# An encoder layer in one kernel: one weight unit of the merges split in front of the first long chunk's fifth job instead of its first

## The chip, the core and the metric

The kernel runs on one core of a Trainium2 chip. The core has a matrix engine (TensorE, PE in the profile; its weight loads are PEld), a vector engine (VectorE, DVE), a scalar engine (ScalarE, ACT), a general engine (GpSimd, POOL) and a queue engine (SyncE, SP) that here does nothing but issue transfers between the chip's memory and the on-chip buffers. Sixteen DMA engines carry the transfers. Each engine takes its instructions strictly in a written order and waits at an instruction until its inputs, and the buffer it writes, are ready.

The metric is the device time of one execution in microseconds, lower is better.

## The reference

One layer of a hybrid encoder over two sequences, a prompt of 1024 tokens and a sample of 2048, each with 16 learned tokens in front, 1024 channels wide, all in float32:

```python
xn = _rmsnorm(h, g_pre)
proj = xn @ w_in + b_in
na_q, na_k, na_v, na_z, ml_qk, ml_v, ml_z, ml_o, ml_g, mg = jnp.split(proj, SPLIT_IDX, axis=-1)
ya = _neighbourhood_attention(na_q, na_k, na_v, na_rpb)
ya = (ya * jax.nn.silu(na_z)) @ w_a
yb = (_mlstm_branch(ml_qk, ml_v, ml_g, ml_o, ml_conv_w, ml_head_g) * jax.nn.silu(ml_z)) @ w_b
ga, gb = jnp.split(jax.nn.sigmoid(mg), 2, axis=-1)
y = (ga * ya + gb * yb) @ w_out
return h + _rmsnorm(y, g_post)
```

So there is one wide input projection; from its columns come a neighbourhood attention on a grid of 64 columns (8 heads of 64) and a bidirectional mLSTM in chunks of 64 tokens (4 heads of 128, with a short convolution in front of its q and k); the two results are gated, projected, mixed and sent through `w_out`.

## The kernel before

**Products.** A float32 matrix is carried as two parts, a high part (`xh`, or the first half of `whl`) and a low part (`xl`, or the second half), and a product is three matmuls: high by high, high by low, low by high. For features on the partitions these are lines 218 to 220, for tokens on the partitions lines 787 to 789.

**Weight units.** The weights come in units of up to 128 x 1056 numbers. On its first use a unit is split: the raw unit is loaded (line 289, `wraw<-wu`, 0.5 MB, two buffers), ACT copies its high part (line 317), DVE subtracts to get the low part (line 318), both into one buffer `whl` of four that go round (`NBW` is 4), and the pair is stored to memory (line 341, `w_...<-whl`, 1 MB). On a later use the stored pair is loaded (line 310, `whl<-w_...`, 1 MB). The number after `w_` only names the stored pair. The core of the split, and the branch for a unit that is split ahead of its use:

```python
both = wp.tile([P, 2, 4 * WU], F32R, name="whl", bufs=NBW)
...
nc.sync.dma_start(both[:, :, :n].bitcast(F32), self.wkept[key])
...
nc.scalar.activation(hi[:, c], raw[:, c], AF.Copy)
nc.vector.tensor_tensor(lo[:, c], raw[:, c], hi[:, c].bitcast(F32), op=ALU.subtract)
...
if key in self.ahead:
    self.wrdy.append(None)
```

A unit that is split ahead is not used by the job that follows: it takes a buffer, is stored, and the buffer is free for the next unit once the store has read it. Such units are the weights of the last stages, here called the merges: the list `MERGE[:-5]`, eleven of them.

**Stages and jobs.** `PLAN` has thirteen dense stages. The first two work on the prompt, the third and fourth on the two halves of the sample ("long chunks" of 1024 tokens; `j` is 2 and 3), then follow the rest of the projections and six merges. A long chunk has nine jobs, `layout("mv")`: two with features on the partitions (four units each: mLSTM q, then mLSTM z), six with tokens on the partitions (two units each: twice 264 columns wide, four times 256), and the mLSTM k's again with four units. `requests` writes the list of units in the order in which they are fetched; in front of some jobs it puts in one unit of the merges.

**Tokens on the partitions.** `tm_unit` takes both units of its job at once and runs tile after tile: 12 matmuls with the first unit (4 blocks of 128 channels by three), then 12 with the second, then DVE adds the bias row `bb` (lines 803 and 805).

**Order.** The dense work above is interleaved with the mLSTM and the attention of the stages already projected. TensorE's order is written out. The orders of DVE, ACT, POOL and SP are set at build time by a scheduler from a model of times; so a changed list of units can also reorder other rows of these engines. Other names used below: `xr<-x_sample` (line 408) loads the sample for its norm, `xsq<-xr` (line 365) sums its squares; `kth` and `ktl` (lines 1577 and 1578) are the two parts of an mLSTM key; `raw<-mk`, `um<-ud`, `gg<-stT`, `to<-stT` and `va<-mv` are loads and stores of the mLSTM and its inputs, `xh<-xh` and `xl<-xl` loads or stores of the two parts of a normed chunk.

Of the kernel before, what the change touches and what calls it, by code (L numbers as in the profile page):

```python
# [57 lines left out]
def _weight_units():  # L58

    return ([("i", x, P) for x in FM_COLS] + [("t", *c, a) for c in TM_COLS for a in range(2)]  # L60
            + [("m", f, P) for f in range(KT)] + [("o", c, a) for c in range(4) for a in range(2)])


def _sw_order(pairs):

    seq = [(pairs[0], "11")]
    for i, p in enumerate(pairs):
        mid = ("22", "s1") if i == 0 else ("s1", "22")
        seq += [(p, o) for o in ("12", "s2", "s3") + mid]
        if i + 1 < len(pairs):  # L70
            seq.append((pairs[i + 1], "11"))
        seq.append((p, "s4"))
    return seq
# [65 lines left out]
class K:  # L139
# [725 lines left out]
    def requests(self):  # L865

        unit = {k: j for j, k in enumerate(_weight_units())}
        ahead = deque(MERGE[:-5])
        self.ahead, first = set(ahead), True
        for j, (s, t0, cols) in enumerate(PLAN):  # L870
            if s == "f":
                assert not ahead
                keys = MERGE[:-5] + [None] * first + MERGE[-5:]
                first = False
            else:
                keys = []
                if "g" not in cols:
                    for n, (kind, c) in enumerate(self.layout(cols)):
                        if ahead and (j == 2 and n < 4 or j == 3 and n):
                            keys.append(ahead.popleft())  # L880
                        keys += [("i", x, P) for x in c] if kind == "fm" else [("t", *c, a) for a in range(2)]
                else:
                    assert not ahead
                    pairs = [p for p in range(14) if "ng"[p > 5] in cols]
                    lead = pairs if (s, t0) not in SW else self.lead(j)
                    keys = [("q", (p, f + "1"), (p, f + "2")) for p in lead for f in "12"]
                    pairs = [p for p in pairs if p not in lead]
                    if pairs:
                        seq = _sw_order(pairs)
                        keys += [("q", *seq[x:x + 2]) for x in range(0, len(seq), 2)]  # L890
            for k in keys:
                if k is None:
                    self.wreq.append(None)
                    continue
                if k[0] == "q":
                    self.wreq.append((k, None, KT, P))
                    continue
                nk, w = (KT, P) if k[0] in "im" else (4, k[2] if k[0] == "t" else 256)
                self.wreq.append((k, self.i["wu"][unit[k], :, :nk * w], nk, w))
# [1307 lines left out]
```

## Time and profile before

| quantity | value |
|---|---|
| median of 3 runs | 2666.21 us (2662.89 to 2666.56) |
| profiled execution | 2665.67 us, span 2663.9 us |
| mean granted TensorE clock | 0.997 |
| PE busy | 2635.1 us, 99% of the span |
| DVE, ACT, POOL busy | 1915.0, 1423.7, 196.3 us |
| memory traffic | 800.47 MB, mean 300 GB/s |

The span runs from the first to the last instruction of the profiled execution. Busy time is counted per engine; an idle engine is of no interest by itself. In the rows of the trace a bracket gives how long the engine was idle before an instruction and what it then waited for. The granted clock is the share of full speed at which TensorE was let run; a value of 0.5 in a short window means that matmuls there took twice as long.

### The profile page before, as it was taken

The page shows a single profiled execution, that of the slowest core. Times are in us where ns is not written, and L with a number is a line of the kernel's source. Part 1 is how long each engine was busy: PE and PEld are TensorE (multiplying, and loading weights), DVE is VectorE, ACT ScalarE, POOL GpSimd, SP SyncE. Part 2 cuts the span into 40 slices and gives each one's busy share as a digit, 9 for nine tenths or more (in the row PEclk, how much of TensorE's full clock was granted, in tenths as well). Part 3 has the DMA queues.
Part 4 walks back from the last instruction along what each step waited for, and adds up shares of the span by engine and source line. Part 5 has one row for each costly group of instructions (what it writes and reads, how often), then busy time and mean ns, then how long its engine had stood idle before and what let it go on. Part 6 is the DMA issues. An engine that isn't in the chain of part 4 may idle for free.

```text
span 2663.9 us, 46683 instructions
## 1 busy us (share of the span) xinstructions
PE 2635.1 (99%) x15928; PEld 2328.5 (87%) x15928; DVE 1915.0 (72%) x5070; ACT 1423.7 (53%) x3292; POOL 196.3 (7%) x418
## 2 busy tenths in 40 slices
PE   9999999999999999999999999999999999999998
PEld 7898897899988999878888888878889898989888
DVE  5655678788776877546676776857478889797854
ACT  5423555555445554546665676656366655656521
POOL 0111131011301124000000000000000000000000
PEclk9999999999999999999999999999999999999999
DMA  9899988799866999978889998899899899898965
GB/s 371 328 332 337 332 302 303 279 339 344 313 218 242 352 324 309 317 230 268 261 269 342 370 295 260 282 348 324 275 323 321 283 306 286 284 306 266 326 244 206
DMA packets 393517, 800.47 MB, mean 300 GB/s; under 512 B 50528, under 2 KB 173360, under 8 KB 389440
## 3 DMA queue, kind: packets, MB, share of 16 engines
q1 hardware_dynamic: 361728, 697.24, 77.9%
q0 software_dynamic: 31552, 100.25, 10.2%
q8 instruction: 126, 2.06, 0.3%
q14 instruction: 111, 0.91, 0.1%
HBM read 543.72 MB, written 253.60 MB: 299 GB/s over the span
## 4 chain that ended last, share of the span: by engine, by line
PE 91%; DMA 4%; DVE 3%; ACT 1%; issue 1%; SPq 0%; DVEq 0%; ACTq 0%
PE pj L218 10%; PE pj L220 10%; PE pj L219 10%; PE pj L988 8%; PE pj L990 8%; PE pj L989 8%; PE pj L787 5%; PE pj L789 5%; PE pj L788 5%; PE pj L1954 3%; PE pj L1953 3%; PE pj L1955 3%; PE sm L1288 3%; PE tr L1273 2%; PE sm L220 1%; PE sm L219 1%
## 5 line engine op out<-in xcount | busy, mean ns | idle before, releaser
L218 PE MATMUL pj<-xh,whl 128*128 128x512 f32 (+1 forms) x960 | 369.7, 385 | 3.1 <-ACT xh L445 2.5
L220 PE MATMUL pj<-xh,whl 128*128 128x512 f32 (+1 forms) x960 | 361.0, 376 | 0.0
L219 PE MATMUL pj<-xl,whl 128*128 128x512 f32 (+1 forms) x960 | 360.3, 375 | 0.2 <-DVE xl L446 0.2
L787 PE MATMUL pj<-whl,xh 128*128 128x256 f32 (+1 forms) x1152 | 329.0, 286 | 0.0
L789 PE MATMUL pj<-whl,xl 128*128 128x256 f32 (+1 forms) x1152 | 325.3, 282 | 0.0
L788 PE MATMUL pj<-whl,xh 128*128 128x256 f32 (+1 forms) x1152 | 324.9, 282 | 0.0
L1953 PE MATMUL pj<-whl,mh 128*128 128x256 f32 x768 | 218.3, 284 | 1.1 <-DMA whl<-w 1.1
L787 PEld LDWEIGHTS pj<-whl,xh 128*128 128x128 f32 x1152 | 217.1, 188 | 0.4
L788 PEld LDWEIGHTS pj<-whl,xh 128*128 128x128 f32 x1152 | 217.0, 188 | 0.2
L789 PEld LDWEIGHTS pj<-whl,xl 128*128 128x128 f32 x1152 | 217.0, 188 | 0.0
L1954 PE MATMUL pj<-whl,mh 128*128 128x256 f32 x768 | 216.3, 282 | 0.0
L1955 PE MATMUL pj<-whl,mlo 128*128 128x256 f32 x768 | 215.5, 281 | 0.0
L218 PEld LDWEIGHTS pj<-xh,whl 128*128 128x128 f32 x960 | 181.2, 189 | 35.3 <-ACT xh L445 3.4
L220 PEld LDWEIGHTS pj<-xh,whl 128*128 128x128 f32 x960 | 181.2, 189 | 35.0
L219 PEld LDWEIGHTS pj<-xl,whl 128*128 128x128 f32 x960 | 181.8, 189 | 30.4 <-issue 1.0
L988 PE MATMUL pj<-xh,whl 128*128 128x512 f32 x512 | 206.7, 404 | 1.3 <-ACT pj L1005 1.1
L990 PE MATMUL pj<-xh,whl 128*128 128x512 f32 x512 | 202.0, 395 | 0.0
L989 PE MATMUL pj<-xl,whl 128*128 128x512 f32 x512 | 201.1, 393 | 0.0
L1280 DVE TENSOR_TENSOR pts<-tr,pts 96x384 fp32r<-96x384 f32 (+2 forms) x192 | 118.6, 618 | 63.8 <-ACT pts L1275 62.4
L1275 ACT ACTIVATE pts<-tr 96x384 fp32r<-96x384 f32 (+2 forms) x192 | 103.5, 539 | 101.7 <-PE tr L1273 101.1
L218 PE MATMUL pj<-yh,whl 128*128 128x512 f32 x384 | 154.1, 401 | 0.0
L219 PE MATMUL pj<-yl,whl 128*128 128x512 f32 x384 | 151.5, 395 | 0.7 <-DVE yl L1855 0.7
(380 smaller groups left out, 6824.9 us busy)
## 6 DMA issues: line engine op xcount, KB each, us to landing
whl<-w SPq DMA_DIRECT2D x131, 1024.0 KB
whl<-q SPq DMA_DIRECT2D x112, 512.0 KB
w<-whl SPq DMA_DIRECT2D x36, 1024.0 KB
wraw<-wu SPq DMA_DIRECT2D x48, 512.0 KB
gt<-st SPq DMA_DIRECT2D x96, 256.0 KB
tg<-gt SPq DMA_DIRECT2D x96, 256.0 KB
q<-po POOLq DMA_DIRECT2D x26, 512.0 KB, 7.3
xt<-xt SPq DMA_DIRECT2D x24, 512.0 KB
```

The lines of the kernel that those rows point to most:

```text
L218: mm(out, ah, bh, start=start, stop=False)
L219: mm(out, ah, bl, start=False, stop=False)
L220: mm(out, al, bh, start=False, stop=stop)
L787: nc.tensor.matmul(o, xh, wh, start=k == 0, stop=False)
L788: nc.tensor.matmul(o, xh, wl, start=False, stop=False)
L789: nc.tensor.matmul(o, xl, wh, start=False, stop=k == KT - 1)
L988: mm(bank, w[:, 0, k], xh[:, k], start=fresh and k == 0, stop=False, skip_group_check=True)
L989: mm(bank, w[:, 0, k], xl[:, k], start=False, stop=False, skip_group_check=True)
L990: mm(bank, w[:, 1, k], xh[:, k], start=False, stop=k == 3, skip_group_check=True)
L1953: nc.tensor.matmul(o, mh[:, k, xs], wh, start=clear > 0 and k == 0, stop=False)
L1954: nc.tensor.matmul(o, mh[:, k, xs], wl, start=False, stop=False)
L1955: nc.tensor.matmul(o, ml[:, k, xs], wh, start=False, stop=clear < 2 and k == KT - 1)
```

## The change

Of the nine jobs of the first long chunk (`j == 2`), four have a merge unit split in front of them. Before, these were the first four jobs; after, they are the second to the fifth. The second long chunk (`j == 3`) keeps its seven. The list of merge units, what is computed from them and the order of TensorE's matmuls stay as they are; the four units are each split one job later.

```diff
@@ -876,7 +876,7 @@
                 keys = []
                 if "g" not in cols:
                     for n, (kind, c) in enumerate(self.layout(cols)):
-                        if ahead and (j == 2 and n < 4 or j == 3 and n):
+                        if ahead and (j == 2 and 0 < n < 5 or j == 3 and n):
                             keys.append(ahead.popleft())
                         keys += [("i", x, P) for x in c] if kind == "fm" else [("t", *c, a) for a in range(2)]
                 else:
```

Two stretches of SP's queue differ by it. The first is the boundary in front of the first long chunk, where a split is taken out; `w_305` is the first unit of that chunk's first job. The piece of the difference:

```order
 L1507 DMA va_2774<-mv_246 128x2x128
-L408 DMA xr<-x_sample 128x1024 x4
+L408 DMA xr<-x_sample 128x1024
+L310 DMA whl<-w_305 128x2x1024
+L408 DMA xr<-x_sample 128x1024 x3
 L415 DMA xt<-xt 128x1024
 L723 DMA nz_151<-st 128x512
-L415 DMA xt<-xt 128x1024
+L1507 DMA va_2774<-mv_246 128x2x128
 L1620 DMA kf<-kf_189 128x256
-L341 DMA w_5198<-whl 256x1x1024
-L289 DMA wraw<-wu 128x1024
```

The store of the split and the raw load of the unit after it are gone from here, and the load of `w_305`, which stood further down, is now the second row behind `va`, among the loads of the sample.

The second stretch is SP's queue around the end of the first long chunk's third job. `w_1411` and `w_1434` are the two units of its fifth job (256 columns). Before:

```order
L310 DMA whl<-w_1411 128x2x1024
L310 DMA whl<-w_1434 128x2x1024
L766 DMA bb<-b_in 128x256
L830 DMA to_257<-stT 128x2x264
L562 DMA xh_512_5658<-xh 128x512
L1437 DMA raw<-mk_207 128x257
L827 DMA gg_259<-stT 128x2x16
L830 DMA to_257<-stT 128x2x248
L562 DMA xh_512_5658<-xh 128x512
L1626 DMA um<-ud_265 128x2x128
L1626 DMA um<-ud_266 128x2x128
L827 DMA gg_259<-stT 128x2x16
```

After, the same stretch begins with these rows:

```order
L310 DMA whl<-w_1411 128x2x1024
L341 DMA w_6986<-whl 256x1x1024
L289 DMA wraw<-wu 128x1024
L766 DMA bb<-b_in 128x256
L830 DMA to_257<-stT 128x2x264
L562 DMA xh_512_5651<-xh 128x512
L827 DMA gg_259<-stT 128x2x16
L830 DMA to_257<-stT 128x2x248
L562 DMA xh_512_5651<-xh 128x512
L1437 DMA raw<-mk_207 128x257
```

and goes on with these, the last rows of the stretch that matter:

```order
L1626 DMA um<-ud_265 128x2x128
L1626 DMA um<-ud_266 128x2x128
L827 DMA gg_259<-stT 128x2x16
L562 DMA xh_512_5651<-xh 128x512
L562 DMA xl_512_5652<-xl 128x512
L830 DMA to_257<-stT 128x2x248
L1507 DMA va_2774<-mv_246 128x2x128
L310 DMA whl<-w_1434 128x2x1024
```

Where the load of `w_1434` stood there are now the store of a split (`w_6986`) and the raw load of the next unit, and the load of `w_1434` stands sixteen rows behind the store, with `raw<-mk_207` halfway. On DVE the split itself comes in at the same place:

```order
-L641 TENSOR_TENSOR xr<-xh,xl 128x1024
-L1657 TENSOR_TENSOR q_6999<-cv,q_6999 128x2x128
-L641 TENSOR_TENSOR xr<-xh,xl 128x1024
+L641 TENSOR_TENSOR xr<-xh,xl 128x1024 x2
+L318 TENSOR_TENSOR whl<-wraw,whl 128x1024
 L805 TENSOR_TENSOR stT<-pj,bb 128x264
 L1673 TENSOR_TENSOR um<-um,trim 128x256
```

The subtraction of line 318 now stands behind both `xr` pieces and ahead of the bias addition, and `q` has moved behind it.

## The prediction

> **What bounds the kernel now.** I read the page's totals first, then TensorE's waits, then the chain of work, and last the rows of the two places where the order differs. Columns of the timeline rows: start in us, duration in us, engine, line, operation, out<-in, shapes; in brackets the idle time before it and its releaser.
>
> ```profile
> span 2663.9 us, 46683 instructions
> PE 2635.1 (99%) x15928; PEld 2328.5 (87%) x15928; DVE 1915.0 (72%) x5070; ACT 1423.7 (53%) x3292; POOL 196.3 (7%) x418
> ```
>
> TensorE is busy for 2635.1 of 2663.9 us, so at most 28.8 us can be won without taking matmuls away, and the change takes none away. DVE, ACT and POOL have slack on average. So a microsecond of the change counts only if it opens or closes an idle gap of TensorE, or alters its clock. The largest waits of TensorE (us in total, times, longest), and below them the one that concerns weights:
>
> ```profile
> PE sm L220 <- DVE ktl L1578: 4.8, 3, 2.6
> PE sc L1703 <- ACT kh L1665: 2.8, 1, 2.8
> ...
> PE pj L218 <- DMA whl<-w: 0.5, 1, 0.5
> ```
>
> Two places matter. The first is the boundary in front of the first long chunk, where the split is taken out; the chain there, then the work that goes, then TensorE's two gaps:
>
> ```profile
> 446.12 8.16 DMA wraw<-wu
> ...
> 454.34 7.53 DMA whl<-w
> ...
> 461.92 0.50 PE pj L218
> ```
> ```profile
> 438.33 1.06 ACT L317 ACTIVATE whl<-wraw 128x1024 fp32r<-128x1024 f32 x1
> ```
> ```profile
> 443.18 1.22 DVE L318 TENSOR_TENSOR whl<-wraw,whl 128x1024 fp32r<-128x1024 f32 x1
> ```
> ```profile
> 440.30 0.39 PE L220 MATMUL sm<-vwh,ktl 128*128 128x260 f32 x1 [2.63 <-DVE ktl L1578]
> ```
> ```profile
> 461.92 0.50 PE L218 MATMUL pj<-xh,whl 128*128 128x512 f32 x1 [0.46 <-DMA whl<-w]
> ```
>
> The chain shows the chunk's first weight load issued at 454.34, behind a raw unit's load, and landing 7.53 us later, 0.46 us too late. The windows around the gap of 2.63 us (columns: window, its length, busy time of PE, PEld, DVE, ACT, POOL, granted clock, DMA share, GB/s):
>
> ```profile
> 437.80:440.20 2.40, 0.00 (x0) 0.00 (x0) 2.40 (x4) 1.90 (x4) 0.00 (x0) 1.00 0.84 246
> 440.70:444.10 3.40, 3.40 (x12) 2.74 (x12) 3.40 (x6) 3.14 (x6) 0.00 (x0) 0.51 0.94 343
> ```
>
> The granted clock was 0.51 for the 3.40 us behind that gap: half of them, 1.7 us, is lost on top of the gap itself.
>
> The second place is between the first long chunk's fourth job (its second 264-wide one) and its fifth (256 wide), around 595 to 625 us, where the split is put in. TensorE has no gap there. Its rows for the first tile of the fifth job, and SP's queue ahead of it:
>
> ```profile
> 617.48 0.28 PE L787 MATMUL pj<-whl,xh 128*128 128x256 f32 x1
> ...
> 618.88 0.28 PE L787 MATMUL pj<-whl,xh 128*128 128x256 f32 x1
> ```
> ```profile
> 594.10 1.29 SPq L310 DMA_DIRECT2D whl<-w  x2
> ...
> 598.17 0.38 SPq L1437 DMA_DIRECT2D raw<-mk  x1
> ...
> 604.95 1.41 SPq L1626 DMA_DIRECT2D um<-ud  x2
> 606.45 1.30 SPq L827 DMA_DIRECT2D gg<-stT  x1
> ...
> 609.78 2.41 SPq L1507 DMA_DIRECT2D va<-mv  x1
> 612.30 2.66 SPq L1437 DMA_DIRECT2D raw<-mk  x1
> ...
> 617.78 0.36 SPq L830 DMA_DIRECT2D to<-stT  x1
> 620.10 0.36 SPq L1626 DMA_DIRECT2D um<-ud  x1
> ```
>
> The job begins at 617.48; its first unit (w_1411) feeds twelve matmuls, so its second unit (w_1434) is needed at 618.88. Both loads were issued at 594.10 to 595.39, more than 23 us ahead. What SP waited for there (us in total, times, longest):
>
> ```profile
> SPq L1626 <- DMA whl<-w: 2.9, 1, 2.9
> ...
> SPq L1626 <- DMA gg<-stT: 1.9, 1, 1.9
> SPq L830 <- DMA um<-ud: 1.7, 1, 1.7
> ```
>
> These three show a rule of this queue that the order bears out: each of SP's transfers goes out only when the one eight places ahead of it has landed. The um of 604.95 stands eight places behind the load of w_1434 and waited for it; the load went out at about 594.8, so it took about 10.1 us. The same reading of the other two gives about 11.9 us (the um pair of 604.95, seen at 617.78) and 13.6 us (the gg of 606.45, seen at 620.10). The transfers are slow because the DMA engines are full:
>
> ```profile
> 600.00:605.00 5.00, 5.00 (x44) 5.00 (x43) 4.57 (x13) 3.13 (x8) 2.11 (x4) 1.00 1.04 391
> 605.00:610.00 5.00, 5.00 (x43) 5.00 (x43) 4.62 (x14) 4.67 (x14) 1.39 (x2) 1.00 1.06 404
> 610.00:615.00 5.00, 5.00 (x44) 5.00 (x43) 4.96 (x16) 3.57 (x10) 2.18 (x4) 1.00 1.00 357
> 615.00:620.00 5.00, 5.00 (x45) 5.00 (x44) 2.31 (x7) 2.13 (x6) 0.00 (x0) 1.00 1.06 392
> ```
>
> **The change part by part.** All splits, loads and stores are still there; four of eleven merge units are taken one job later, so only the ends of the moved stretch differ: one split less at the boundary, one more at the second place. The matmul order is the same.
>
> *At the boundary* go 1.06 us of ACT, 1.22 us of DVE, a store of 1 MB and a raw load of 0.5 MB. The chunk's first load moves up in SP's queue, past the raw load and among the four loads of x_sample, so it lands some 15 us ahead of its use and the wait of 461.92 closes: -0.46. The gap of 440.30 stays, because what holds it stands ahead of the removed rows:
>
> ```profile
> 437.56 2.36 DVE L542 TENSOR_TENSOR xl<-xt,xh 128x1024 fp32r<-128x1024 f32 x2
> 439.83 0.42 DVE L1578 TENSOR_TENSOR ktl<-tr,kth 128x256 fp32r<-128x256 f32 x1
> ```
>
> ktl runs at 439.83 behind two xl pieces, ahead of the removed DVE row at 443.18. What the earlier weight load pushes back is the x_sample loads, for which ACT already waits:
>
> ```profile
> 440.77 1.06 ACT L365 ACTIVATE xsq<-xr 128x1024 bf16<-128x1024 f32 x1 [1.06 <-DMA xr<-x_sample]
> ```
>
> 1 MB at the window's 343 GB/s takes 3.1 us; TensorE waits for these squares only through the rows behind them on ACT (a kth and a kh), so the bounds are 0 and about +3; I take 0, since no wait of TensorE on ACT is shown in this stretch.
>
> *At the second place* come 1.06 us of ACT and 1.22 us of DVE, both beside a TensorE that is busy in all of every window above; they cost nothing while that cover lasts. The DMAs are what counts. The split's buffer is one of four, and w_1434's load now takes the buffer that the split leaves: it is issued only when the store of the split has gone out and, by its new place in SP's queue, behind the va transfer that was issued at 609.78. I follow the eight-place rule:
>
> The split's DVE half stands behind two xr subtractions, the second of which is this row:
>
> ```profile
> 594.30 1.22 DVE L641 TENSOR_TENSOR xr<-xh,xl 128x1024 f32<-128x1024 f32 x1
> ```
>
> With the split behind it, and one 0.4 us row fewer ahead of it, the split ends near 596.4, where the store is issued. The transfer eight places behind the store is a raw<-mk; it goes out when the store has landed, 10.1 us later (the row of the 1 MB load), at 606.5. Eight places behind that raw<-mk stands w_1434's load. If that small transfer needs 10.1 to 11.9 us (the first two readings above), the load goes out at 616.6 to 618.4. Its own landing takes 7.53 (chain, boundary) to 10.1 us. So it lands at 624.1 to 628.5, against a need of 618.88: a stall of 5.2 to 9.6 us, where TensorE has nothing else to run in its written order. The lower bound of the whole: only the place in the queue counts, the issue is at 612.3 when va has gone out (609.78 and 2.41), and the landing takes 7.53: 619.8, a stall of 0.9. The upper bound of the whole takes the 13.6 of the third reading: issue at 620.1, landing at 630.2, a stall of 11.3. I take 7.5, near the middle of 5.2 and 9.6, because the three readings of this very stretch all show 10 us or more, and 1.5 MB more enters it.
>
> *Clock.* A gap of 2.63 us was followed by 3.4 us at 0.51; a stall of 7.5 us brings at least that, +1.7; two such stretches, +3.4, are the bound above, 0 the one below.
>
> *Behind it.* DVE, ACT and the DMAs go on while TensorE stands, so the next small wait of the same kind goes:
>
> ```profile
> 672.30 0.38 PE L220 MATMUL sm<-vwh,ktl 128*128 128x260 f32 x1 [0.98 <-DVE ktl L1578]
> ```
>
> It has a shift of 7 us to its good: -0.98. The other changes of order, around 1508 to 1583 and at 1787 us, swap neighbouring rows in stretches where TensorE shows no gap: 0. If their cover goes, each would be of the size of the wait just shown, 1 us.
>
> Sum: -0.46 + 7.5 + 1.7 - 0.98 = +7.8 us. The profiled execution's time is 2665.67, 1.8 above its span and 0.5 under the median of 2666.21. That gives 2673.5.
>
> **The rivals.**
>
> *The load comes in time.* For: the issue at 612.3 is possible if the store and the raw<-mk land fast; then a landing in 6.5 us or less meets 618.88. Against: no 1 MB load among the rows above was that quick. TensorE then loses nothing: -0.46, and the 0.98 stays; 2665.2. If the stall is only the lower bound, 0.9, the time is 2666.1. The Trainium skill, DMA: Bandwidth & Descriptors, in Measured under Bandwidth, has 6.15 us for a load of 1 MB; by it the load would land at 618.5 and this rival would hold. The trace's 7.53 and 10.1 us in a full stretch speak against it.
>
> *Faster.* The first gap closes: if ktl of 439.83 ran 2.4 us or more earlier, 2.63 and the 1.7 us of half clock would go with the 0.46, and with a second split that is hidden and the 0.98 gone the time would be 2659.9. Against: ktl's row and the two xl rows ahead of it stand in the same order as before, and the ACT row that goes starts at 438.33, behind the kth it reads.
>
> *Longer.* The upper bounds together: a stall of 11.3 and 3.4 for the clock, which with the two gains of 0.46 and 0.98 is +13.3, so 2678.9. For it: the small gg transfer did need 13.6 us. Against: SP's queue is itself held up in the changed kernel, and fewer transfers stand in each other's way then.
>
> **How the numbers follow.** Chances: a stall of 5.2 to 9.6 us with one stretch of half clock 0.58; the load in time or less late than that 0.25; longer 0.12; faster 0.05. The forecast's own range is 2671 to 2676 (the sum with a stall of 5.2 is +5.5, with 9.6 it is +9.9). The range for 8 in 10 reaches into both neighbours: 2666 (a stall of 0.9) to 2679. A measurement of this kernel tells about 0.2%, 5.3 us, from no change, so slower means above 2671.5 and faster under 2660.9. Of the main case a twentieth ends below 2671.5, and the rival of the timely load lies within: slower 0.67, within 0.28, faster 0.05.
>
> **What would show it.** Right: a wait of L787 on whl<-w of several us at about 618.9, followed by some 3.4 us at a clock near 0.5; w_1434's load issued after 612; no wait at 461.9; the gap of 2.63 at 440.3 as before; the wait near 672 gone. Wrong: no gap at 618.9 (the landing under 7 us, or the buffer free earlier than the store), or a new wait of TensorE at the boundary on ACT's squares, or a missing half clock behind a long stall.

## The result and the profile after

The changed kernel takes 2679.82 us (median of 4 runs, 2674.1 to 2682.82), the kernel before 2665.7 us on the same chip. The ratio is 1.0051, with a 95% interval of 1.0037 to 1.0065: 13.6 us slower by that ratio, 10 to 17 us by its interval (the two medians lie 14.1 us apart). The forecast was 2673.5 with a range up to 2679.0; the direction and the place were right, and the time lies 0.8 us above the range.

The profiled execution took 2681.11 us. Its totals, on the page of the changed kernel:

```profile
span 2679.0 us, 46680 instructions
...
PE 2640.2 (99%) x15928; PEld 2332.1 (87%) x15928; DVE 1913.3 (71%) x5070; ACT 1423.8 (53%) x3292; POOL 195.5 (7%) x418
```

The engines do as much as before; TensorE's busy time is 5 us longer, and its idle time 10 us. The largest waits of TensorE (us in total, times, longest):

```profile
PE pj L787 <- DMA whl<-w: 8.2, 2, 7.5
PE sm L220 <- DVE ktl L1578: 5.5, 5, 2.6
...
PE pj L787 <- DVE stT L805: 0.9, 1, 0.9
```

A wait of line 787 on a weight load heads the list, which was not there before. TensorE's rows at the places that the forecast spoke of:

```profile
440.22 0.59 PE L220 MATMUL sm<-vwh,ktl 128*128 128x260 f32 x1 [2.64 <-DVE ktl L1578]
...
455.47 0.33 PE L218 MATMUL sm<-vwh,kth 16*128 16x130 f32 x1 [0.43 <-ACT kth L1577]
...
456.25 0.32 PE L220 MATMUL sm<-vwh,ktl 16*128 16x130 f32 x1 [0.34 <-DVE ktl L1578]
...
462.16 0.39 PE L218 MATMUL pj<-xh,whl 128*128 128x512 f32 x1
...
592.84 0.39 PE L787 MATMUL pj<-whl,xh 128*128 128x264 f32 x1 [0.66 <-DMA whl<-w]
...
598.60 0.39 PE L787 MATMUL pj<-whl,xh 128*128 128x264 f32 x1 [0.91 <-DVE stT L805]
...
629.01 0.58 PE L787 MATMUL pj<-whl,xh 128*128 128x256 f32 x1 [7.53 <-DMA whl<-w]
...
634.10 0.41 PE L787 MATMUL pj<-whl,xh 128*128 128x256 f32 x1
...
684.27 0.39 PE L220 MATMUL sm<-vwh,ktl 128*128 128x260 f32 x1 [0.20 <-DVE ktl L1578]
...
699.24 0.39 PE L220 MATMUL sm<-vwh,ktl 128*128 128x260 f32 x1 [1.06 <-DVE ktl L1578]
...
2652.90 0.39 PE L1953 MATMUL pj<-whl,mh 128*128 128x256 f32 x1 [1.28 <-DMA whl<-w]
```

The same matmuls in the kernel before, where the prediction does not show them already:

```profile
591.87 0.28 PE L787 MATMUL pj<-whl,xh 128*128 128x264 f32 x1
...
596.27 0.28 PE L787 MATMUL pj<-whl,xh 128*128 128x264 f32 x1
...
621.58 0.28 PE L787 MATMUL pj<-whl,xh 128*128 128x256 f32 x1
...
686.05 0.28 PE L220 MATMUL sm<-vwh,ktl 128*128 128x260 f32 x1
...
2637.86 0.39 PE L1953 MATMUL pj<-whl,mh 128*128 128x256 f32 x1 [1.06 <-DMA whl<-w]
```

TensorE runs the same matmuls in the same order, so the shift of one matmul between the two traces is what has been lost up to it. Between the last two rows it is 15.04 us, nearly all of the difference of the spans, 15.1. Step by step:

| up to the matmul of | shift so far | step | what the row of the changed kernel shows |
|---|---|---|---|
| 461.92 before, 462.16 after | +0.24 | +0.24 | the wait of 0.46 is gone, two of 0.43 and 0.34 (kth, ktl) are new |
| 591.87, 592.84 | +0.97 | +0.73 | a wait of 0.66 on a load of the fourth job |
| 596.27, 598.60 | +2.33 | +1.36 | a wait of 0.91 on a bias addition on DVE |
| 618.88, 629.01 | +10.13 | +7.80 | the stall, 7.53 |
| 621.58, 634.10 | +12.52 | +2.39 | matmuls at half clock |
| 672.30, 684.27 | +11.97 | -0.55 | the ktl wait there is 0.20, it was 0.98 |
| 686.05, 699.24 | +13.19 | +1.22 | a new ktl wait, 1.06 |
| 2637.86, 2652.90 | +15.04 | +1.85 | small waits in the long rest |

The windows of the stall (columns as in the prediction):

```profile
621.50:624.40 2.90, 0.00 (x0) 0.00 (x0) 0.96 (x2) 0.51 (x2) 0.00 (x0) 1.00 1.09 303
624.40:629.00 4.60, 0.00 (x0) 0.00 (x0) 0.60 (x1) 0.19 (x1) 0.00 (x0) 0.50 0.99 306
629.00:634.60 5.60, 5.59 (x26) 5.59 (x27) 1.36 (x5) 1.97 (x5) 0.00 (x0) 0.50 0.93 350
634.60:640.00 5.40, 5.40 (x47) 5.40 (x47) 4.64 (x15) 2.42 (x7) 1.06 (x2) 1.00 0.89 317
```

The clock fell to 0.50 while TensorE stood, and stayed there for 5.6 us after it had begun to run again. The chain behind the stall, then SP's rows (the store of the split, the raw<-mk eight places behind it, the um eight places ahead of the last row shown, va, the load of w_1434, and that last row), then three of SP's waits (us in total, times, longest):

```profile
606.85 13.01 DMA raw<-mk
619.87 9.09 DMA whl<-w
```
```profile
598.22 0.51 SPq L341 DMA_DIRECT2D w<-whl  x1
...
606.85 0.33 SPq L1437 DMA_DIRECT2D raw<-mk  x1
608.08 0.96 SPq L1626 DMA_DIRECT2D um<-ud  x2
...
618.30 1.17 SPq L1507 DMA_DIRECT2D va<-mv  x1
619.87 0.58 SPq L310 DMA_DIRECT2D whl<-w  x1
623.50 0.33 SPq L1437 DMA_DIRECT2D raw<-mk  x1
```
```profile
SPq L1437 <- DMA w<-whl: 2.3, 1, 2.3
...
SPq L1507 <- DMA xh<-xh: 0.9, 1, 0.9
...
SPq L310 <- DMA raw<-mk: 0.4, 1, 0.4
```

The links of the forecast are there: store, raw<-mk, load. The store went out at 598.22 (forecast 596.4), the raw<-mk at 606.85 (606.5), the load at 619.87 (616.6 to 618.4); it landed at 629.0 (624.1 to 628.5). SP waited 2.3 us for the store before it could issue the raw<-mk, so the store took 8.6 us and not 10.1; the raw<-mk took 13.0 us and not 10.1 to 11.9. But the raw<-mk alone held the load back by only 0.4 us: SP was done with the row ahead of the load, va, at 619.47, since its other rows had waited for landings too (va for an xh). The need had moved from 618.88 to 621.5, by the waits ahead of it, so the stall came out at 7.53.

### The profile page after: what moved, and what is told of

It reads as the page before. It is cut to its first block, busy times and chain, and to the rows that moved or that the text cites. A ratio compares the mean times of both kernels' runs of the same rounds, so it can differ in the third digit from the quotient of the medians.

```text
span 2679.0 us, 46680 instructions
## 1 busy us (share of the span) xinstructions
PE 2640.2 (99%) x15928; PEld 2332.1 (87%) x15928; DVE 1913.3 (71%) x5070; ACT 1423.8 (53%) x3292; POOL 195.5 (7%) x418
## 3 DMA queue, kind: packets, MB, share of 16 engines
q0 software_dynamic: 31552, 100.25, 10.1%
## 4 chain that ended last, share of the span: by engine, by line
PE 84%; DMA 9%; DVE 4%; ACT 2%; issue 1%; SPq 0%; DVEq 0%; POOL 0%; ACTq 0%
PE pj L218 9%; PE pj L220 9%; PE pj L219 9%; PE pj L988 8%; PE pj L990 8%; PE pj L989 8%; PE pj L787 4%; PE pj L789 4%; PE pj L788 4%; PE pj L1954 3%; PE pj L1953 3%; PE pj L1955 3%; PE sm L1288 2%; PE tr L1273 2%; DMA wraw<-wu 1%
```

## The experiments

Two theories stood against each other. A: the load of w_1434 goes out late, because SP's transfers each wait for the one eight places ahead, and that sets the stall. B: the bytes in flight set it, wherever the load stands. Ratios are to the kernel before on the same chip, with 95% intervals.

**The changed kernel again.** No edit.

> The changed kernel once more, for a second profile and a time beside the experiments. If the stall in front of the fifth job comes from the order of SP's queue, its row is there again with 6 to 9 us, followed by 3.4 to 7 us of running at half clock, and the time is 2674 to 2683. If it came from a chance of that one execution, the stall is under 3 us in the second profile.

Measured: 1.0051 (1.0038 to 1.0063). The stall's row:

```profile
627.42 0.58 PE L787 MATMUL pj<-whl,xh 128*128 128x256 f32 x1 [7.23 <-DMA whl<-w]
```

The stall is there again, and so is the wait of 0.9 us on the bias addition (597.31); the wait of 0.66 on the fourth job's load is only 0.07. So that last one is not a fixed part of the change. From the same matmuls as in the table, this execution lost 10.2 us: -0.3 up to the chunk's first matmul, 1.3 from there to 596.27, 7.5 for the stall, 2.2 at half clock, 0.2 in the two ktl waits behind it, and -0.7 in the long rest.

**The split is not stored.**

```diff
+                    if key == MERGE[3]:
+                        self.wkept[key] = self.wkept[MERGE[2]]
+                    else:
+                        self.hold.append((d, both[:, :, :n].bitcast(F32)))
-                    self.hold.append((d, both[:, :, :n].bitcast(F32)))
```

> As the changed kernel, but the unit split in front of the fifth job is not stored (the merges read another unit's stored pair in its place, so the output is not the reference's); its raw load and the split on ACT and DVE stay. The buffer is free at once, and the load of w_1434 stands two rows behind that of w_1411 again. Theory A (the late load costs the stall, the stall the clock): no stall near 621, no half clock behind it, PE's small waits near 592 and 598 stay; some 10 us less than the changed kernel, 2668 to 2671. Theory B (the DMA engines are full, and the raw load and the rest still come too late): a stall of 3 us or more remains, 2674 or more. Theory C (the split's work on ACT and DVE is the cost): hardly changed, 2677 to 2680.

Measured: 1.0002 (0.9993 to 1.0011), the time of the kernel before. TensorE's clock and busy time where the stall was:

```profile
618.00:624.00 6.00, 6.00 (x54) 6.00 (x53) 3.06 (x9) 3.73 (x9) 0.00 (x0) 1.00 0.92 295
624.00:630.00 6.00, 6.00 (x54) 6.00 (x53) 6.00 (x16) 2.31 (x8) 1.06 (x2) 1.00 0.93 303
```

No stall and no half clock. The time is lower than theory A said (2668 to 2671): with the stall go not only the half clock, but also the waits behind it. The wait on the bias addition remains:

```profile
596.77 0.39 PE L790 MATMUL pj<-whl,xh 128*128 128x264 f32 x1 [0.90 <-DVE stT L808]
```

So the work on ACT and DVE (theory C) costs about 0.9 us by this row, and nothing that the time can tell; all else hangs on the store and on the load behind it. The run takes away both the chain and 1 MB, and does not tell A from B.

**The addition alone.**

```diff
-                        if ahead and (j == 2 and 0 < n < 5 or j == 3 and n):
+                        if ahead and (j == 2 and n < 5 or j == 3 and n > 1):
```

> The addition alone: the first long chunk has five splits, in front of its first to fifth job, and the second chunk one fewer (none in front of its second job), so the boundary is as before. By theory A the loss is that of the second place alone: the stall of some 7.5 us and the half clock, as in the changed kernel, and the wait of 0.46 us near 462 is there again: 2677 to 2682. If the boundary's new order had cost something (theory D), this kernel is 2 us or more faster than the changed one.

Measured: 1.0052 (1.0039 to 1.0064), a stall of 7.17. (The second chunk has one split fewer here, so that the list of units still comes out.) The boundary as it was before neither helps nor hurts by an amount that can be told: the loss is that of the second place. In this profile the boundary's wait was 1.80 us, against 0.46 in the profile of before, so it varies from one execution to the next by more than the 0.46 that the forecast took off.

**The load issued by ACT.**

```diff
-                nc.sync.dma_start(both[:, :, :n].bitcast(F32), self.wkept[key])
+                first = key == ("t", C_MV, 256, 1) and not hasattr(self, "moved")
+                queue = nc.scalar if first else nc.sync
+                if first:
+                    self.moved = True
+                queue.dma_start(both[:, :, :n].bitcast(F32), self.wkept[key])
```

> As the changed kernel, but the one load of w_1434 in the first long chunk is issued by ACT instead of SP, so that it waits for its buffer (the store of the split) and for ACT's own rows ahead of it, and not for the transfers ahead of it in SP's queue. All bytes are moved as in the changed kernel. In the changed kernel the ACT rows around it ran at 613 to 614. Theory A (its place in SP's queue and the wait for the transfer eight places ahead): issued near 613, landing near 622, a stall of 0 to 2 us and little or no half clock, 2668 to 2673. Theory B (full DMA engines): it lands hardly earlier than 629, since the same bytes are in flight, and the time stays at 2677 or more.

Measured: 1.0036 (1.0024 to 1.0049). Both theories missed how it went. The chain of this kernel, and what ACT waited for from 600 to 632 us:

```profile
607.73 12.19 DMA raw<-mk
619.93 9.98 DMA whl<-w
```
```profile
ACT hb L1764 <- DMA raw<-mk: 6.2, 1, 6.2
```

ACT reached the load at about 614.4 and then stood for 5.5 us until the raw<-mk, a transfer of SP's queue, had landed (the 6.2 of the view includes the issue); the load went out at 619.93, at the same time as from SP. So the count of eight is not SP's own: SP and ACT share it. The traces show what is counted: in all fifteen profiles the transfers of SP and ACT report their landing on eight semaphores (counters on which engines wait), taken strictly in turn, so each waits until the one eight places ahead has given its semaphore back. The profiled execution has a stall of 7.31 and was the slowest of the five (2677.75 us, median 2673.85); what made the others quicker no trace shows.

**The load issued by POOL.** The edit is the same with `nc.gpsimd`.

> As the changed kernel, but the one load of w_1434 in the first long chunk is issued by POOL, behind its two stores of t01, which in the changed kernel went out at 608.40 and 609.65. Issued by ACT it still waited for the landing of the same raw transfer as in SP's queue and went out at 619.93, so SP and ACT share the count of eight; POOL's transfers go by another queue (the software one of the page). All bytes are moved as in the changed kernel. Theory A (the count of eight makes it late): issued near 610.5, landing near 619.5 by the 9.1 us that it took, against a need near 621: no stall above 1 us and no half clock, 2668 to 2672. Theory B (the full DMA engines make it late): it lands after 625 all the same, and the stall is 4 us or more, 2674 or more.

Measured: 1.0001 (0.9992 to 1.0010): all of the loss is gone, with every byte still moved. POOL's row and TensorE's:

```profile
608.96 0.73 POOL L314 DMA_DIRECT2D whl<-w  x1
```
```profile
621.77 0.39 PE L791 MATMUL pj<-whl,xh 128*128 128x256 f32 x1 [1.59 <-DMA whl<-w]
```

The load went out 10.9 us earlier than from SP and landed 7.2 us earlier, after 12.8 us. A stall of 1.59 is left, with no half clock behind it. That is close to theory A's time (2667.15 us, against 2668 to 2672); the landing is slower than A assumed. The run takes the load out of SP's queue altogether, so it frees it from the count of eight and from the transfers ahead of it in that queue alike.

**The low half on POOL.**

```diff
-                    nc.vector.tensor_tensor(lo[:, c], raw[:, c], hi[:, c].bitcast(F32), op=ALU.subtract)
+                    engine = nc.gpsimd if key == MERGE[3] else nc.vector
+                    engine.tensor_tensor(lo[:, c], raw[:, c], hi[:, c].bitcast(F32), op=ALU.subtract)
```

> As the changed kernel, but the subtraction of the unit that is split in front of the fifth job is done by POOL instead of DVE. If the wait of 0.9 us near 598 comes from that subtraction standing ahead of a bias addition on DVE, it is gone; the stall stays, since the store waits for POOL instead and goes out no earlier. The time is within 2 us of the changed kernel, 2676 to 2682; if POOL takes several us for it, the stall grows by as much.

Measured: 1.0040 (1.0027 to 1.0053). The wait on the bias addition did not go, it grew to 1.66 us. POOL's row, and DVE's beside it:

```profile
592.38 2.39 POOL L319 TENSOR_TENSOR whl<-wraw,whl 128x1024 fp32r<-128x1024 f32 x1 [12.71 <-ACT whl L317]
```
```profile
592.72 2.33 DVE L1654 SCALAR_TENSOR_TENSOR cv<-th,cv 128x256 f32<-128x256 f32 x1
```

The DVE row that ran beside POOL's took 2.33 us; the same row took 0.41 in the kernel before. POOL's work was paid for by DVE. Here the load went out at 614.87, 5 us earlier than in the changed kernel, and still landed at 628.4, with a stall of 7.80: this speaks against theory A.

**The same split one job later.**

```diff
+                        if ahead and (j == 2 and n in (1, 2, 3, 5) or j == 3 and n):
```

> The split that the change puts in front of the fifth job stands in front of the sixth instead (second, third, fourth and sixth). In SP's order its store then stands right behind the load of w_1701 and 17 rows ahead of that of w_1724, the second unit of the sixth job: the same pattern one job later. Theory A: the same stall one job later, 5 to 9 us and the half clock, 2674 to 2682. If it was the special load of the DMA engines around 600 to 625 (theory B), this place, where the DMAs were less busy in the kernel before (252 and 315 GB/s from 620 to 630), has a stall under 3 us, 2668 to 2671.

Measured: 1.0022 (1.0013 to 1.0031). The same pattern, one job later and smaller (the profiled execution took 2680.73 us and was the slowest of eleven, whose median is 2672.65):

```profile
650.72 0.58 PE L787 MATMUL pj<-whl,xh 128*128 128x256 f32 x1 [4.18 <-DMA whl<-w]
```

**In front of the second chunk's first job.**

```diff
+                        if ahead and (j == 2 and 0 < n < 4 or j == 3):
```

> The split stands in front of the second long chunk's first job instead (second to fourth job of the first chunk, all jobs of the second). This keeps what the change does at the boundary and undoes the second place. The units around it belong to the first job, which takes four units at once; its store stands in SP's order between the loads of w_305 and w_323. If the place in front of the fifth job is all that costs, the time is that of the kernel before less the 0.5 us of the boundary, 2663 to 2666; if a split in front of any job of this kind stalls TensorE, there is a new wait on whl<-w at the start of the second chunk, near 880 us at the latest, and 3 us or more are lost.

Measured: 1.0027 (1.0017 to 1.0038). Not the place in front of the fifth job alone stalls TensorE:

```profile
784.43 0.76 PE L218 MATMUL pj<-xh,whl 128*128 128x512 f32 x1 [3.96 <-DMA whl<-w]
```

The load that TensorE waited for stands only seven rows behind the store here. It went out when the load of the job's first unit, eight places ahead, had landed, and then took 14.35 us itself:

```profile
761.52 8.36 DMA whl<-w
769.95 14.35 DMA whl<-w
```

**In front of the seventh, the eighth, the ninth job.** The same line, with 6, 7 or 8 for the 5.

> The split of the fifth job in front of the seventh. In SP's order the load of that job's second unit stands 11 rows behind the store, against 16 and 17 for the fifth and sixth. By theory A the load waits for a transfer that itself did not have to wait for the store's landing (it stands eight ahead of the load and three behind the store): one landing of some 10 us instead of two, so a stall under 3 us, 2665 to 2670. If every job with two units stalls alike, 2673 or more.

> The split of the fifth job in front of the eighth. In SP's order the load of that job's second unit stands only five rows behind the store, so by theory A it waits for nothing but the landing of the store (its buffer): no stall or one under 1 us, 2663 to 2667, the least of all places. If every job with two units stalls alike, 2673 or more.

> The split of the fifth job in front of the ninth, which has features on the partitions and takes four units. In SP's order the second unit's load stands nine rows behind the store, eight behind the raw load that follows the store. By theory A the load waits for that one landing, some 10 us, and for the buffer: a stall of 0 to 3 us, 2664 to 2669. If a job of four units cannot run ahead of its units, a stall as in front of the second chunk's first job, 4 us and the half clock, 2671 to 2675.

Measured: 1.0013 (1.0004 to 1.0021), 1.0015 (1.0005 to 1.0025) and 1.0004 (0.9996 to 1.0013). None of the three has a stall on the load of a second unit, as the count of rows between store and load said (16 and 17 rows: stalls; 11, 5 and 9: none). The count is no rule beyond these places, since in front of the second chunk 7 rows came with a stall. But the seventh and the eighth are still 3 to 4 us slower than before. In the profile of the eighth a wait is larger that the split does not touch:

```profile
676.73 0.39 PE L220 MATMUL sm<-vwh,ktl 128*128 128x260 f32 x1 [3.06 <-DVE ktl L1578]
```

It was 0.98 before. What lengthens it was not tried. In front of the ninth job the split costs nothing that can be told, and gains nothing: the kernel before is not beaten.

**One transfer more ahead of the load.**

```diff
+                if key == ("t", C_MV, 256, 1) and not hasattr(self, "moved"):
+                    self.moved = True
+                    tiny = wp.tile([1, 16], F32, name="tiny", bufs=1)
+                    nc.sync.dma_start(tiny, self.wkept[MERGE[3]][0:1, 0, 0:16])
                 nc.sync.dma_start(both[:, :, :n].bitcast(F32), self.wkept[key])
```

> As the changed kernel, but one transfer of 64 bytes is put in SP's queue right ahead of the load of w_1434. It moves next to nothing; it only shifts the count of eight by one, so that the load waits for an um<-ud transfer instead of the raw<-mk. In the changed kernel that raw<-mk had landed at 619.87, and the um (issued at 608.08) only at 623.50, where a later row of SP waited for it. Theory A (the count of eight): the load goes out 3.6 us later and lands 3.6 us later, so the stall is near 11 us instead of 7.5, and the time 2 to 5 us above that of the changed kernel, 2680 to 2686. Theory B (only the bytes in flight count): no difference, a stall of 7 to 8 us, 2676 to 2682.

Measured: 1.0044 (1.0032 to 1.0056), a miss for A's number. What SP waited for, its row, and TensorE's:

```profile
SPq L314 <- DMA um<-ud: 1.9, 1, 1.9
```
```profile
616.69 0.57 SPq L314 DMA_DIRECT2D whl<-w  x1
```
```profile
627.60 0.58 PE L791 MATMUL pj<-whl,xh 128*128 128x256 f32 x1 [7.72 <-DMA whl<-w]
```

The load did wait for the um instead, so one transfer of 64 bytes changed what it waits for; that is the count of eight. But this um had landed in 10.6 us, not in 15, so the load went out 3.2 us earlier and not later. And it landed after 10.9 us, 1.4 us earlier than in the changed kernel and no earlier than in that one's second execution (issued at 619.45, landed at 627.4).

**A sixteenth of the store.**

```diff
+                    if key == MERGE[3]:
+                        self.wkept[key] = self.wkept[MERGE[2]]
+                        self.hold.append((d[:, :, :64], both[:, :, :64].bitcast(F32)))
+                    else:
+                        self.hold.append((d, both[:, :, :n].bitcast(F32)))
-                    self.hold.append((d, both[:, :, :n].bitcast(F32)))
```

> As the changed kernel, but of the unit split in front of the fifth job only a sixteenth is stored (64 of 1024 columns of each half; the merges read another unit's stored pair in its place, so the output is not the reference's). The number of transfers stays, 0.94 MB fewer are moved; in SP's order the load of w_1434 changes places with the va transfer, so it waits for the landing of an xh transfer, which in the changed kernel came at about 618.2, 1.7 us ahead of the raw<-mk's. If the count of eight alone makes the load late, and each transfer takes as long as before, the load goes out near 618 and the stall is 5 to 7 us, the time 2675 to 2680. If the bytes in flight set how long the transfers take, 0.94 MB at some 400 GB/s is 2.4 us less for those in front of the load and for the load itself, the stall is 2 to 4 us, and the time 2669 to 2674. If nearly all of it is the bytes of the store, there is no stall, as without the store, 2664 to 2668.

Measured: 1.0023 (1.0014 to 1.0032), a stall of 3.98, as the bytes said. The load in the chain:

```profile
610.42 14.74 DMA whl<-w
```

SP came to the load at 610.42, 9.5 us earlier than in the changed kernel, and it landed 14.7 us later, at 625.2: 3.8 us earlier. Of 9.5 us won at the issue, 5.7 were lost in flight.

## Why the forecast had the place and the stall right and the sum too small

**The boundary, -0.46: wrong by a little, measured +0.24 (-0.29 in the second execution).** The wait on the first load closed as forecast, and the gap of 2.63 at 440.30 stayed as forecast (2.64). But two waits of 0.43 and 0.34 on kth and ktl came in its place at 455 and 456, the kind that the bounds of 0 to +3 for ACT's rows allowed and the sum set to 0. Run with the boundary as before, the loss is the same, so this term is too small to tell.

**The split's work on ACT and DVE, 0: wrong, measured 0.9.** The prediction said that it costs nothing beside a busy TensorE. In the changed kernel the subtraction stands ahead of a bias addition, and TensorE waited for that addition. The cover was not TensorE's busy time, but how soon DVE empties TensorE's result buffers. A wait of 0.4 to 0.9 us stands there in all kernels with DVE's split at that place (0.90 without the store), 1.66 where POOL did it, and not in those with the split in front of a later job.

**The stall, 7.5: right in size, 7.53, and 7.23 in a second execution, in part by luck.** The place, the wait and the links store, raw<-mk and load were named. A stall of 7.5 had the load land at 626.4; it landed at 629.0, half a microsecond behind the latest of the forecast's main case. The need came 2.6 us later too, so the two errors cancel. (One reading of the prediction is short, too: the later um of the pair went out at 605.40 and landed at 617.71, so it took 12.3 us and not 11.9.) The picture of a load that lands a fixed time after it is issued was too simple: 1 MB took 7.4 to 14.7 us in flight, and mostly the longer the earlier it went out (7.4 from 621.6 in the kernel with the addition alone, 9.1 from 619.9, 10.9 from 616.7, 13.5 from 614.9, 14.7 from 610.4). The semaphores of the traces show what lies behind this. Leaving aside the one of 64 bytes, each of SP's transfers in this stretch landed after the one issued before it. In the seven profiles with this load on SP or ACT it landed 2.1 to 3.2 us behind the transfer ahead of it, whether it went out at 610.4 or at 621.6. So an earlier issue mostly means a longer wait behind the same transfers.

Both theories hold a part. The count of eight decides when the load goes out (shown by what ACT and, with one more transfer, SP waited for); the transfers still ahead of it decide what an earlier issue is worth (1.4 us of 3.2, 3.8 of 9.5). Only a load on POOL's queue, issued 10.9 us earlier, brought most of it back: issued at 608.96, it landed at 621.73, before two of SP's transfers that had been issued ahead of it (606.98, landed at 622.86, and 608.34, at 624.66). How the transfers in flight share the engines stays open. The Trainium skill, DMA: Bandwidth & Descriptors, in Queues, rings and completion order, says that each DMA engine goes round between the queues that have work; that fits the gain of POOL's queue, but no run here shows it by itself. The figure of 6.15 us for 1 MB, which the prediction set beside the rival without a stall, was not met by any of these loads; a later load of the kernel before, issued at 621.19, had landed at 627.13.

**The clock, 1.7: too small, measured 2.4.** The prediction took the 3.4 us that followed the gap of 2.63. The kernel before had a longer stretch, behind a gap of 2.81 at 1799.80:

```profile
1799.30:1806.00 6.70, 6.04 (x19) 5.13 (x20) 4.09 (x12) 4.68 (x14) 0.00 (x0) 0.50 0.81 276
```

In all fifteen profiles a stretch at half clock lasts 3.41, 6.83 or 10.24 us, so one, two or three times the same step, unless the end of the program cuts it off. In the changed kernel it was 10.24, beginning 2.9 us into the stall; 5.6 us of it lay behind the stall, which costs half of that, 2.8 by the window (2.39 by the rows up to 634.10). In the second execution it was 6.83, with 4.6 us behind the stall. So the price varies by half a microsecond with the place in these steps at which the stall ends.

**The wait at 672, -0.98: measured -0.55, and +1.22 directly behind it.** The wait shrank to 0.20, but another of the same kind came at 699. In the second execution both were there again, with 0.21 and 0.86. Without the store, and with the load on POOL, the new one was not there. But in front of the seventh and the eighth job ktl waits of 1.95 and 3.06 us came without any stall, so the stall is not the only thing that brings them.

**The other reorderings, 0: measured +1.85 after 699,** in small waits, none above 0.7 at one place that was not there before. The second execution has -0.7 for its rest, and 0.07 where the first has 0.73 on the fourth job's load. What part of these belongs to the change stays open.

So the step that failed is the pricing of what lies around the stall: five terms summed to +0.3 in the forecast (-0.46, 0, 1.7, -0.98 and 0) and to +7.2 in the trace (the 15.04 less the 7.80). Three of them missed in both executions: the split's work, priced at nothing, showed a wait of 0.9 on a bias addition; the clock, priced at 1.7, cost 2.2 to 2.4; and the wait behind, priced as a gain of 0.98, came out as a loss of 0.2 to 0.7, since the new one outweighed what the old one lost. The small waits of the rest differ between the executions, and their cause stays open; but the loss as a whole is no chance of one set of runs, as the second set has the same ratio. The range reached to 2679 through a longer stall, and had nothing for several small waits at once.

## What to carry to other kernels

A transfer that is added in front of a load can delay it twice: it holds the buffer, and it pushes the load behind others that must land first; look at the rows ahead of it in the queue, since here it landed only when they had, however early it was issued. A stall of several us brings its surroundings with it, the clock and new waits where engines had been in step: here 13.6 us in all for a stall of 7.2 to 7.5. Work put on an engine with idle time is hidden only if nothing that the bounding engine waits for stands behind it.

## What the runs showed of the hardware

- ACT's and SP's transfers shared one count of eight (eight semaphores, used in turn in all fifteen profiles): a load issued by ACT stood 5.5 us for a transfer of SP's.
- In this stretch SP's transfers landed in the order of their issue: 1 MB loads took 7.4 us when issued at 621.6 and 14.7 when issued at 610.4, and landed 2.1 to 3.2 us behind the transfer ahead of them. A load on POOL's queue overtook two of SP's.
- A POOL subtraction of 128x1024 (2.39 us) stretched the DVE row beside it from 0.41 to 2.33 us.
- The gap of about 2.64 us at 440 was followed by half clock in thirteen of fifteen profiles. Half clock lasted 3.41, 6.83 or 10.24 us in all of them; after the stall it reached 5.6 us into the running.
